# In each group of eight expert matmuls, the second expert goes first

## The chip, the cores and the metric

The kernel runs on one core of one Trainium2 chip. The metric is the device time of one execution in microseconds (us). Most executions of this kernel agree within 0.3%.

## The reference

A first block (token mixer, then a mixture of experts with 32 experts, 4 per token) is followed by a second block of two layers, whose feed-forward is a lookup over 16384 experts. Only the mixture of experts matters here. For 256 tokens of width 1024 in float32, cut down:

```
logits = yf @ router_w + router_b
top_val, top_idx = lax.top_k(logits, TOP_K)          # 4 of 32
gates = softmax(top_val)
def expert_block(xb, e):
    gt = minimum(xb @ w_gate[e] + b_gate[e], 7.0)
    up = clip(xb @ w_up[e] + b_up[e], -7.0, 7.0)
    return (gt * sigmoid(1.702 * gt) * (up + 1.0)) @ w_down[e] + b_down[e]
out = sum over the chosen experts of gate * expert_block
```

Each of `w_gate`, `w_up` and `w_down` is 1024 x 1024 for each expert: 12.6 MB an expert, 402.7 MB in all, read once.

## The kernel before

The generator `moe` holds the expert stage. Experts are taken in pairs. Each expert has up to `CAP` = 64 token slots; `xg` holds the gathered tokens, transposed. One expert alone therefore needs 64 of the array's 128 columns. The two experts of a pair share one PSUM bank `ps_g`: expert 0 writes partitions 0 to 63 from the left half of the array's columns (tile position (0, 0)), expert 1 partitions 64 to 127 from the right half ((0, 64)).

A weight tile `mo` is 128 x 2048 float32 (1 MB): 4 chunks of the contraction by 512 outputs of one matrix of one expert. It is loaded by `expert_load` (line 529, on SP's queue) into a ring of four buffers. A **group** is the work on two such tiles, one of each expert: eight matmuls, the two experts in turn, four chunks each. A pair of experts has 8 groups for gate and up (line 1055) and 4 for down (line 1089), so there are 192 groups, 384 weight tiles, 1536 matmuls. A float32 matmul stands as two MATMUL instructions in the profile, so these are 3072 there (2048 of line 1055 and 1024 of line 1089), and a pair of equal rows "x2" is one matmul of the program.

The order on every engine comes from the list scheduler that builds the program. It plays the program through on its own timeline and gives an engine the ready instruction of the best priority. While the expert stage runs, other work has a lower priority (the `filler` contexts): matmuls in float32r over all 128 columns for the context half of the second block, lines 209 to 211, 150 to 152, 671, 789, 897, 898 and 900. They are issued where the expert work is not ready by the scheduler's own times. Their weights come through SP's queue too (`wr`, lines 136 and 832), are split by ScalarE (`wh`, line 117) and VectorE (`wl`, line 118), and are used from there.

SP's queue runs in order: the load into a ring buffer waits until the last matmul that reads the buffer is done, and everything behind it in the queue waits too.

Of the kernel before, what the change touches and what calls it, by code (L numbers as in the profile page):

```python
# [64 lines left out]
def kernel(ctx: ExitStack, tc: tile.TileContext, a: dict, out: bass.AP):  # L65
# [88 lines left out]
    def xs_tiles(name, shape=None):  # L154
        h = xs.tile([P, KD * T], F32R, tag="xh", name=name + "h", bufs=2)
        l = xs.tile([P, KD * T], F32R, tag="xl", name=name + "l", bufs=2)
        return h, l
# [126 lines left out]
        nc.vector.tensor_add(b_, b_, h_)  # L284
        return gb

    # ---------------------------------------------------------------- modulation vectors of the second block
    modt = [[cp.tile([P, 2, 16], F32, name=f"modt{l}{q}") for q in range(3)] for l in range(2)]
    mrow = [[dr.tile([2, 2 * D], F32, name=f"mrow{l}{q}") for q in range(3)] for l in range(2)]

# [64 lines left out]
            return bank  # L355
        return f

    # ---------------------------------------------------------------- phase 1: attention of the first block
    X = xs_tiles("x")
    rp = pool("route", side="right")  # L360
    mg_stack = ctx.enter_context(ExitStack())
# [226 lines left out]
    for k2 in range(4):  # L588
        yb = ytr(k2)
        for c in range(2):  # L590
            k = 2 * k2 + c
# [89 lines left out]

    mg_stack.close()

    # ---------------------------------------------------------------- expert lookup layer: top-k, weights, dense passes
    def top16(rows):
        for s_, m_, _ in rows:
            nc.vector.max(m_[:, 0:8], s_)
        for s_, m_, x_ in rows:
            nc.vector.max_index(x_[:, 0:8], m_[:, 0:8], s_)
        for s_, m_, _ in rows:  # L690
            nc.vector.match_replace(s_, m_[:, 0:8], s_, LOWEST)
        for s_, m_, _ in rows:
            nc.vector.max(m_[:, 8:16], s_)
        for s_, m_, x_ in rows:
            nc.vector.max_index(x_[:, 8:16], m_[:, 8:16], s_)
# [229 lines left out]

    gds = [[dr.tile([P, 8, P, 16], F32, name=f"gd{i}{b}") for b in range(2)] for i in range(3)]

    # ---------------------------------------------------------------- experts of the first block
    def moe(mo, res):
        ahead = True  # L930
        lg = rp.tile([P, 2, 32], F32, name="lg")
# [76 lines left out]
        for g4 in range(8):  # L1008
# [11 lines left out]
            for k2 in range(4):  # L1020
                bank = psum("g").rearrange("p (c s) -> p c s", c=2)
                for c in range(2):
                    k = 2 * k2 + c
# [4 lines left out]
                for c in range(2):  # L1028
                    k = 2 * k2 + c
                    nc.scalar.activation(xg[:, k, :], bank[:, c, :], AF.Identity, bias=lnc[:, 1, k:k + 1], scale=lnc[:, 0, k:k + 1])  # L1030
            for p2 in range(2):
                e0 = 4 * g4 + 2 * p2
                selv = []
                for mi in range(2):
                    sel = mo.tile([P, 2, CAP], F32R, tag="sel", name="sel", bufs=4)
                    nc.vector.tensor_copy(sel, identr[:, 32 * mi + e0:32 * mi + e0 + 2, None].to_broadcast([P, 2, CAP]))
                    selv.append(sel.rearrange("p e s -> p (e s)"))
                if todo:
                    todo.pop()()
                hdn = mo.tile([P, D], F32, tag="hdn", name="hdn")  # L1040
                for hf in range(2):
                    banks = []
                    for mi, w in enumerate(("w_gate", "w_up")):
                        bank = psum("g")
                        for kq in range(2):
                            wt = []
                            for i in range(2):
                                if not (ahead and moq):
                                    res["last"] = expert_load(a[w][e0 + i, hf, kq])
                                    ahead = False  # L1050
                                wt.append(moq.pop(0))
                            for k in range(4):
                                for i in range(2):
                                    o = (2 * p2 + i) * CAP
                                    nc.tensor.matmul(bank[64 * i:64 * i + 64, :], xg[:, kq * 4 + k, o:o + CAP], wt[i][:, k, :],  # L1055
                                                     start=(kq == 0 and k == 0), stop=False, skip_group_check=True,
                                                     tile_position=(0, 64 * i))
                        nc.tensor.matmul(bank, selv[mi], bgr[:, hf * 512:hf * 512 + 512], start=False, stop=True,
                                         skip_group_check=True)
                        banks.append(bank)  # L1060
                    gt = mo.tile([P, 512], F32, tag="gt", name="gt", bufs=2)
                    nc.vector.tensor_scalar(gt, banks[0], 7.0, None, op0=ALU.min)
                    sg = mo.tile([P, 512], F32, tag="sg", name="sg", bufs=1)
                    nc.scalar.activation(sg, gt, AF.Sigmoid, scale=1.702)
                    up = mo.tile([P, 512], F32, tag="up", name="up", bufs=1)
                    nc.vector.tensor_scalar(up, banks[1], 7.0, -7.0, op0=ALU.min, op1=ALU.max)
                    nc.vector.tensor_mul(gt, gt, sg)
                    nc.vector.scalar_tensor_tensor(hdn[:, hf * 512:(hf + 1) * 512], up, 1.0, gt, op0=ALU.add, op1=ALU.mult)
                    yield
                if todo:  # L1070
                    todo.pop()()
                hT = mo.tile([P, KD, P], F32, tag="hT", name="hT", bufs=1)
                for c2 in range(2):
                    tp = psum("g").rearrange("p (c s) -> p c s", c=4)
                    for c in range(4):
                        k = 4 * c2 + c
                        nc.tensor.transpose(tp[:, c, :], hdn[:, k * P:(k + 1) * P], ident)
                    nc.scalar.activation(hT[:, 4 * c2:4 * c2 + 4, :], tp, AF.Copy)
                yo = mo.tile([P, D], F32, tag="y", name="yo")
                for hf in range(2):  # L1080
                    bank = psum("g")
                    for kq in range(2):
                        wt = []
                        for i in range(2):
                            res["last"] = expert_load(a["w_down"][e0 + i, hf, kq])
                            wt.append(moq.pop(0))
                        for k in range(4):
                            for i in range(2):
                                nc.tensor.matmul(bank[64 * i:64 * i + 64, :], hT[:, kq * 4 + k, 64 * i:64 * i + 64], wt[i][:, k, :],  # L1089
                                                 start=(kq == 0 and k == 0), stop=(kq == 1 and k == 3), skip_group_check=True,  # L1090
                                                 tile_position=(0, 64 * i))
                    nc.scalar.activation(yo[:, hf * 512:(hf + 1) * 512], bank, AF.Copy)
                tp = psum("g")
                pt_ = mo.tile([P, T], F32, tag="pt", name="pt", bufs=2)
                for tb in range(2):
                    nc.tensor.transpose(tp[:, tb * P:(tb + 1) * P], og[tb][:, 2 * p2:2 * p2 + 2, :].rearrange("p e s -> p (e s)"), ident)
                nc.scalar.activation(pt_, tp[:, 0:256], AF.Copy)
                for tb in range(2):
                    for hf in range(2):
                        bank = psum("g")  # L1100
                        nc.tensor.matmul(bank, pt_[:, tb * P:(tb + 1) * P], yo[:, hf * 512:(hf + 1) * 512], start=True, stop=True)  # L1101
                        nc.vector.tensor_add(acc[:, tb, hf * 512:(hf + 1) * 512], acc[:, tb, hf * 512:(hf + 1) * 512], bank)
                yield
# [67 lines left out]
    mo = pool("moe", stack=moe_stack)  # L1171
    mres = {}
    mgen = moe(mo, mres)
    next(mgen)
    general("g")
# [66 lines left out]
    moe_stack.close()  # L1242
    mow_stack.close()

    # ---------------------------------------------------------------- second block, first layer, latent tokens
    am_stack = ctx.enter_context(ExitStack())
    am = pool("amix", stack=am_stack)
    HA = xs_tiles("ha")
# [41 lines left out]
    vs_stack.close()  # L1290
    ra_stack.close()

    # ---------------------------------------------------------------- second block, second layer
    gl_stack = ctx.enter_context(ExitStack())
    gl = pool("gla", stack=gl_stack)
    wm_stack = ctx.enter_context(ExitStack())
# [248 lines left out]
            nc.sync.dma_start(out[:, tb, s_], o)  # L1545


# [1 line left out]
def consts():  # L1549
    p=np.arange(128)[:,None]; c=np.arange(128)[None,:]  # L1550
    ident=(p==c).astype(np.float32)
# [9 lines left out]
        tabs.append(np.where(ok,d,np.float32(1e30)).astype(np.float32))  # L1561
    return np.ascontiguousarray(np.concatenate([ident,iota,lt,gt,ones,trif,trib]+tabs,1))
def nt(w,n0=None):
    # [K,N] -> [N/128][128 p][K/128*128]
    K,N=w.shape
    return np.ascontiguousarray(w.reshape(K//128,128,N//128,128).transpose(2,1,0,3).reshape(N//128,128,K))
def tn(w,nw=512):
    # [K,N] -> [N/nw][K/256][128][2*nw]
    K,N=w.shape
    return np.ascontiguousarray(w.reshape(K//256,2,128,N//nw,nw).transpose(3,0,2,1,4).reshape(N//nw,K//256,128,2*nw))  # L1570
def xT(x):
# [3 lines left out]
def layout(i):  # L1575
# [10 lines left out]
    o['w_v1']=tn(np.ascontiguousarray(v[:,512:]),384)[0]  # L1586
    o['w_g']=np.stack([nt(ga),nt(gb)])
    o['sinks']=i['sinks']
    pa=i['w_proj_a'][0] # [256,1024] -> [2][128][4n][2k][128]
    o['w_pa']=np.ascontiguousarray(pa.reshape(2,128,2,4,128).transpose(2,1,3,0,4).reshape(2,128,1024))  # L1590
    o['w_pb']=nt(np.ascontiguousarray(i['w_proj_b'][0][perm]))
    o['w_out']=tn(i['w_out'][0])
# [55 lines left out]
```

## Time and profile before

| what | value |
|---|---|
| runs | 4312.46, 4317.56, 4323.53 us; median 4317.56 us |
| span of the profiled execution, first to last instruction | 4312.5 us |
| TensorE (PE) busy | 4173.2 us, 97% |
| VectorE (DVE), ScalarE (ACT) busy | 2385.2 us (55%), 1934.8 us (45%) |
| expert matmuls, lines 1055 and 1089, busy | 571.4 us and 289.7 us |
| first and last expert matmul starts | 309.7 us and 2237.8 us |

For the profiled execution the table has its span; that is within 0.1 us of the lowest run and 5.1 us below the median, and a time around the span is not shown apart from it. "PE busy" is the time in which at least one matmul is in the array. Matmuls overlap, so the start of one to the start of the next says what a matmul costs, and its own length does not.

### The profile page before, as it was taken

To read this page: it belongs to the slowest core of one execution; us is meant where nothing else is said; L and a number is where in the kernel's file an instruction comes from. 1 tells how busy PE (TensorE), PEld (TensorE's weight loads), DVE (VectorE), ACT (ScalarE), POOL (GpSimd) and SP (SyncE) were. 2 spreads that over 40 slices of the span, in tenths; PEclk is the share of its full clock that TensorE was granted. 3 is DMA by queue.
4 is the path that set the end of the run, shared out by engine and by line. 5 is a ranking of instruction groups with operands and counts; after the bars stand their busy time and mean duration, and the time that the engine had idled before them with its cause. 6 is when DMAs were issued, how large, how long until landed. Compare 5 with 4: busy or idle time off the path is not lost.

```text
span 4312.5 us, 63252 instructions
## 1 busy us (share of the span) xinstructions
PE 4173.2 (97%) x23786; PEld 3087.1 (72%) x23786; DVE 2385.2 (55%) x6357; ACT 1934.8 (45%) x2838; POOL 165.8 (4%) x230
## 2 busy tenths in 40 slices
PE   8999989999999999999998999999998989999998
PEld 7675545566565565656557999878877689988887
DVE  4364686433333333333337897655455689865555
ACT  5542246433232233323324497445544538754443
POOL 0000012000000000000000012000000002200000
PEclk9999999999999999999999999999998999999999
DMA  7658778887878878787875567876774345787773
GB/s 255 236 208 330 294 290 320 316 309 295 310 281 315 321 298 308 287 317 286 310 265 185 188 223 266 289 277 215 255 273 159 107 155 206 261 299 239 232 237 131
DMA packets 340046, 1115.49 MB, mean 259 GB/s; under 512 B 28934, under 2 KB 128006, under 8 KB 283672
## 3 DMA queue, kind: packets, MB, share of 16 engines
q1 hardware_dynamic: 323896, 1043.22, 67.5%
q10 hardware_dynamic: 15552, 66.07, 3.9%
q8 instruction: 190, 3.11, 0.3%
q0 software_dynamic: 288, 2.10, 0.1%
q14 instruction: 120, 0.98, 0.1%
HBM read 1041.97 MB, written 69.30 MB: 258 GB/s over the span
## 4 chain that ended last, share of the span: by engine, by line
PE 76%; DVE 5%; ACT 2%; DMA 2%; issue 1%; POOL 0%; SPq 0%; ACTq 0%; DVEq 0%; POOLq 0%
PE ps_g L1055 11%; PE ps_a L898 8%; PE ps_a L897 8%; PE ps_a L900 8%; PE ps_u L150 7%; PE ps_u L152 7%; PE ps_u L151 7%; PE ps_g L1089 6%; PE ps_a L789 3%; PE ps_g L1101 1%; DVE wl L118 1%; PE ps_g L329 1%; PE ps_g L209 1%; PE ps_g L210 1%; PE ps_g L211 1%; DVE o L788 1%
## 5 line engine op out<-in xcount | busy, mean ns | idle before, releaser
L118 DVE TENSOR_TENSOR wl<-wr,wh 128x1024 fp32r<-128x1024 f32 x933 | 1132.2, 1222 | 1126.6 <-ACT wh L117 1108.1
L117 ACT ACTIVATE wh<-wr 128x1024 fp32r<-128x1024 f32 x933 | 978.9, 1054 | 1379.1 <-PE ps_u L151 580.5
L898 PE MATMUL ps_a<-wl,ah 128*128 128x512 f32 x1536 | 590.5, 399 | 3.1 <-DVE wl L118 3.1
L1055 PE MATMUL ps_g<-mo,xg 128*64 128x512 f32 x2048 | 571.4, 603 | 10.0 <-DMA mo<-in_w_gate_dram 5.9
L897 PE MATMUL ps_a<-wh,ah 128*128 128x512 f32 x1536 | 577.6, 398 | 0.0
L900 PE MATMUL ps_a<-wh,al 128*128 128x512 f32 x1536 | 481.1, 396 | 0.0
L1055 PEld LDWEIGHTS ps_g<-mo,xg 128*64 128x64 f32 x2048 | 155.1, 137 | 286.6 <-issue 252.3
L897 PEld LDWEIGHTS ps_a<-wh,ah 128*128 128x128 f32 x1536 | 288.0, 188 | 85.2 <-issue 20.0
L898 PEld LDWEIGHTS ps_a<-wl,ah 128*128 128x128 f32 x1536 | 286.6, 188 | 82.3 <-issue 18.6
L900 PEld LDWEIGHTS ps_a<-wh,al 128*128 128x128 f32 x1536 | 286.4, 188 | 80.8 <-issue 16.4
L151 PE MATMUL ps_u<-xbl,wh 128*128 128x256 f32 x1088 | 315.4, 290 | 0.0
L150 PE MATMUL ps_u<-xbh,wh 128*128 128x256 f32 x1088 | 314.4, 289 | 0.0
L152 PE MATMUL ps_u<-xbh,wl 128*128 128x256 f32 x1088 | 313.7, 288 | 0.0
L1089 PE MATMUL ps_g<-mo,hT 128*64 128x512 f32 x1024 | 289.7, 605 | 2.4 <-DMA mo<-in_w_down_dram 2.4
L150 PE MATMUL ps_u<-xah,wh 128*128 128x256 f32 x960 | 276.5, 288 | 2.7 <-ACT sp L859 2.7
L152 PE MATMUL ps_u<-xch,wl 128*128 128x256 f32 x960 | 274.1, 287 | 4.2 <-DVE wl L118 4.2
L152 PE MATMUL ps_u<-xah,wl 128*128 128x256 f32 x960 | 274.5, 288 | 3.4 <-DVE wl L118 3.4
L151 PE MATMUL ps_u<-xal,wh 128*128 128x256 f32 x960 | 276.1, 288 | 0.0
L150 PE MATMUL ps_u<-xch,wh 128*128 128x256 f32 x960 | 274.5, 286 | 0.3 <-ACT wh L117 0.3
L151 PE MATMUL ps_u<-xcl,wh 128*128 128x256 f32 x960 | 274.6, 286 | 0.0
L788 DVE TENSOR_SCALAR o<-cst,it 128x128 f32<-128x128 f32 x768 | 233.7, 345 | 28.7 <-PE ps_a L789 28.2
L150 PEld LDWEIGHTS ps_u<-xbh,wh 128*128 128x128 f32 x1088 | 206.8, 190 | 48.3 <-issue 44.8
(652 smaller groups left out, 7028.1 us busy)
## 6 DMA issues: line engine op xcount, KB each, us to landing
wr<-in_p_u_dram SPq DMA_DIRECT2D x384, 512.0 KB, 4.6
wr<-in_p_v_dram SPq DMA_DIRECT2D x384, 512.0 KB, 4.5
mo<-in_w_gate_dram SPq DMA_DIRECT2D x128, 1024.0 KB, 7.1
mo<-in_w_up_dram SPq DMA_DIRECT2D x128, 1024.0 KB, 6.7
mo<-in_w_down_dram SPq DMA_DIRECT2D x128, 1024.0 KB, 7.1
gd<-stg ACTq DMA_DIRECT2D x48, 1024.0 KB, 6.2
gr<-gd SPq DMA_DIRECT2D x96, 512.0 KB, 7.0
mw<-in_w_mod_dram SPq DMA_DIRECT2D x48, 512.0 KB, 4.2
```

The source lines that it names most:

```text
L117: nc.scalar.activation(h, src, AF.Copy)
L118: return nc.vector.tensor_sub(l, src, h.bitcast(F32)).ins
L150: nc.tensor.matmul(o, wh, xh, start=first, stop=False)
L151: nc.tensor.matmul(o, wh, xl, start=False, stop=False)
L152: nc.tensor.matmul(o, wl, xh, start=False, stop=last)
L788: nc.vector.tensor_scalar(o1, iota, it[:, 0, t:t + 1], it[:, 2, t:t + 1], op0=ALU.is_equal, op1=ALU.mult)
L789: nc.tensor.matmul(bank[:, 2 * i2 + i, :], o2q[:, i, :], o1, start=True, stop=True)
L897: nc.tensor.matmul(acc[tb][hf], ah[:, ts], wh[:, hs], start=first, stop=False)
L898: nc.tensor.matmul(acc[tb][hf], ah[:, ts], wl[:, hs], start=False, stop=False)
L900: nc.tensor.matmul(acc[tb][hf], al[:, ts], wh[:, hf * 512:(hf + 1) * 512], start=False, stop=fin)
L1055: nc.tensor.matmul(bank[64 * i:64 * i + 64, :], xg[:, kq * 4 + k, o:o + CAP], wt[i][:, k, :], start=(kq == 0 and k == 0), stop=False, skip ...
L1089: nc.tensor.matmul(bank[64 * i:64 * i + 64, :], hT[:, kq * 4 + k, 64 * i:64 * i + 64], wt[i][:, k, :], start=(kq == 0 and k == 0), stop=(k ...
```

## The change

In both places the inner loop over the two experts is turned round. The loads, their order in the code, the products and the sums stay. (The rest of the diff takes comments out.)

```diff
@@ -1050,7 +1050,7 @@
                             for k in range(4):
-                                for i in range(2):
+                                for i in (1, 0):
                                     o = (2 * p2 + i) * CAP
                                     nc.tensor.matmul(bank[64 * i:64 * i + 64, :], xg[:, kq * 4 + k, o:o + CAP], wt[i][:, k, :],
@@ -1085,7 +1085,7 @@
                         for k in range(4):
-                            for i in range(2):
+                            for i in (1, 0):
                                 nc.tensor.matmul(bank[64 * i:64 * i + 64, :], hT[:, kq * 4 + k, 64 * i:64 * i + 64], wt[i][:, k, :],
```

Since the scheduler decides the order, the program changes more than the two lines do. On TensorE, in a group of the gate matrix early in the stage, `mo_3090` is the tile of the first expert, whose load is issued first, and `mo_3092` that of the second. Before:

```order
L1055 MATMUL ps_g_3089<-mo_3090,xg_2985 64x512
L209 MATMUL ps_a_3575<-wh_3614,hch_3465 128x512
L210 MATMUL ps_a_3575<-wl_3615,hch_3465 128x512
L211 MATMUL ps_a_3575<-wh_3614,hcl_3466 128x512
L1055 MATMUL ps_g_3089<-mo_3092,xg_2985 64x512
L1055 MATMUL ps_g_3089<-mo_3090,xg_2985 64x512
L1055 MATMUL ps_g_3089<-mo_3092,xg_2985 64x512
L1055 MATMUL ps_g_3089<-mo_3090,xg_2985 64x512
L1055 MATMUL ps_g_3089<-mo_3092,xg_2985 64x512
L1055 MATMUL ps_g_3089<-mo_3090,xg_2985 64x512
L1055 MATMUL ps_g_3089<-mo_3092,xg_2985 64x512
```

Now:

```order
L209 MATMUL ps_a_3575<-wh_3614,hch_3465 128x512
L210 MATMUL ps_a_3575<-wl_3615,hch_3465 128x512
L211 MATMUL ps_a_3575<-wh_3614,hcl_3466 128x512
L1055 MATMUL ps_g_3089<-mo_3092,xg_2985 64x512
L1055 MATMUL ps_g_3089<-mo_3090,xg_2985 64x512
L1055 MATMUL ps_g_3089<-mo_3092,xg_2985 64x512
L1055 MATMUL ps_g_3089<-mo_3090,xg_2985 64x512
L1055 MATMUL ps_g_3089<-mo_3092,xg_2985 64x512
L1055 MATMUL ps_g_3089<-mo_3090,xg_2985 64x512
L1055 MATMUL ps_g_3089<-mo_3092,xg_2985 64x512
L1055 MATMUL ps_g_3089<-mo_3090,xg_2985 64x512
```

The first expert's first matmul stood alone ahead of three matmuls of other work; it now stands with the other seven, at their place. The last matmul of the group now reads the first expert's tile.

In a group of the down matrix on TensorE (line 1089), `mo_5208` is the first expert's tile, `mo_5210` the second's, and line 789 is filler. Before:

```order
L1089 MATMUL ps_g_5207<-mo_5208,hT_5193 64x512
L789 MATMUL ps_a_8719<-o1_8736,o2_8730 128x128
L1089 MATMUL ps_g_5207<-mo_5210,hT_5193 64x512
L1089 MATMUL ps_g_5207<-mo_5208,hT_5193 64x512
L1089 MATMUL ps_g_5207<-mo_5210,hT_5193 64x512
```

Now:

```order
L1077 MATMUL ps_g_5200<-cst_75,hdn_5072 128x128 x4
L1089 MATMUL ps_g_5207<-mo_5210,hT_5193 64x512
L1089 MATMUL ps_g_5207<-mo_5208,hT_5193 64x512
L1089 MATMUL ps_g_5207<-mo_5210,hT_5193 64x512
L1089 MATMUL ps_g_5207<-mo_5208,hT_5193 64x512
```

The single filler matmul that parted the group stands elsewhere, and the group is whole. Over the whole program, the expert matmuls stand on TensorE in these uninterrupted runs (counted in the built order, in matmuls of the program):

| length of a run | 1 | 4 | 7 | 8 | 9 | 12 | 15 | 16 | 17 | 24 | runs |
|---|---|---|---|---|---|---|---|---|---|---|---|
| before | 141 | 0 | 143 | 24 | 3 | 0 | 2 | 8 | 1 | 0 | 322 |
| now | 0 | 5 | 0 | 169 | 0 | 5 | 0 | 5 | 0 | 1 | 185 |

TensorE has the same instructions as before, in another order, and outside the expert stage (the first 1748 rows and the last 11612 of 20877) the same order. The number of filler matmuls between the end of a group and the start of the next but one has the same median, 64. On SP's queue the two loads of a group stand side by side in 179 of 192 groups, before in 185.

## Rows read from the trace of the kernel before

**Rows 1.** The page: span, and part 1 (busy time and share).

```profile
span 4312.5 us, 63252 instructions
PE 4173.2 (97%) x23786; PEld 3087.1 (72%) x23786; DVE 2385.2 (55%) x6357; ACT 1934.8 (45%) x2838; POOL 165.8 (4%) x230
```

**Rows 2.** Busy time by stretch: length, engines with instructions, clock, DMA share, GB/s.

```profile
core 0: us, PE busy (x) PEld busy (x) DVE busy (x) ACT busy (x) POOL busy (x), PEclk, DMA share, GB/s
309.00:2242.00 1933.00, 1893.08 (x9328) 1107.14 (x9328) 798.90 (x2060) 661.49 (x923) 49.02 (x69) 0.99 0.81 305
309.00:460.00 151.00, 151.00 (x704) 85.75 (x705) 72.17 (x97) 47.08 (x57) 3.72 (x3) 1.00 0.84 323
460.00:800.00 340.00, 308.86 (x1603) 171.45 (x1598) 244.46 (x1360) 165.15 (x330) 45.30 (x67) 0.96 0.80 304
800.00:2000.00 1200.00, 1196.36 (x5893) 715.77 (x5893) 408.43 (x515) 380.34 (x451) 0.00 (x0) 1.00 0.82 305
```

**Rows 3.** Waits in the expert stage, all engines: us in total, times, longest us.

```profile
ACT wh L117 <- PE ps_u L151: 407.4, 107, 10.8
...
ACT wh L117 <- PE ps_a L900: 236.2, 90, 7.1
```

**Rows 4.** Timeline of PE around three groups: start us, us, instruction, count.

```profile
1106.31 3.65 PE L1089 MATMUL ps_g<-mo,hT 128*64 128x512 f32 x16
1109.89 0.39 PE L150 MATMUL ps_u<-xbh,wh 128*128 128x256 f32 x1
...
1111.30 0.28 PE L152 MATMUL ps_u<-xbh,wl 128*128 128x256 f32 x1
1111.42 0.28 PE L150 MATMUL ps_u<-xbh,wh 128*128 128x256 f32 x1
1111.63 1.07 PE L1089 MATMUL ps_g<-mo,hT 128*64 128x512 f32 x2
1112.63 0.38 PE L151 MATMUL ps_u<-xbl,wh 128*128 128x256 f32 x1
...
1114.29 0.28 PE L152 MATMUL ps_u<-xbh,wl 128*128 128x256 f32 x1
1114.50 3.65 PE L1089 MATMUL ps_g<-mo,hT 128*64 128x512 f32 x14
1118.07 0.39 PE L150 MATMUL ps_u<-xbh,wh 128*128 128x256 f32 x1
```

**Rows 5.** Timeline of PE: first and last lone matmul, last run of seven.

```profile
324.88 1.07 PE L1055 MATMUL ps_g<-mo,xg 128*64 128x512 f32 x2
...
2209.33 1.07 PE L1055 MATMUL ps_g<-mo,xg 128*64 128x512 f32 x2
...
2210.76 3.65 PE L1055 MATMUL ps_g<-mo,xg 128*64 128x512 f32 x14
```

**Rows 6.** The page, part 5: expert matmuls, busy us, mean ns, idle before.

```profile
L1055 PE MATMUL ps_g<-mo,xg 128*64 128x512 f32 x2048 | 571.4, 603 | 10.0 <-DMA mo<-in_w_gate_dram 5.9
...
L1089 PE MATMUL ps_g<-mo,hT 128*64 128x512 f32 x1024 | 289.7, 605 | 2.4 <-DMA mo<-in_w_down_dram 2.4
```

**Rows 7.** Waits of PE alone in the expert stage, for weight tiles.

```profile
PE ps_g L1055 <- DMA mo<-in_w_gate_dram: 5.9, 3, 3.9
...
PE ps_g L1055 <- DMA mo<-in_w_up_dram: 3.1, 3, 2.1
...
PE ps_g L1089 <- DMA mo<-in_w_down_dram: 2.4, 2, 1.6
```

**Rows 8.** Timeline of SP's queue: issues of weight tiles around the same groups.

```profile
1098.62 1.17 SPq L529 DMA_DIRECT2D mo<-in_w_down_dram  x2
...
1109.98 0.81 SPq L529 DMA_DIRECT2D mo<-in_w_down_dram  x2
...
1117.33 1.17 SPq L529 DMA_DIRECT2D mo<-in_w_down_dram  x2
```

**Rows 9.** The view of the tile `mo`: its transfers, issue to landing.

```profile
DMA to landing us min/median/max: 4.7/7.0/11.5
```

## The prediction

> **What bounds the kernel now.** I began with the page's busy shares: TensorE works 97% of the span and no other engine more than 55% [rows 1]. A mean hides stages, so I cut the span at the expert stage next. It takes 1933 us, and TensorE is busy in 1893 of them; between 800 and 2000 us it is idle for 3.6 of 1200, at a granted clock of 1.00, which is the 2.4 GHz level [rows 2]. The reader is to see that in this stretch only less work on TensorE, or a fuller array, can shorten the time. The waits say the same from the other side: ScalarE's split of the next filler weights stands idle until TensorE has freed a buffer, 407.4 and 236.2 us of the stage [rows 3], so that chain runs ahead of TensorE and is not what TensorE waits for. TensorE's own waits for expert weights come to 11.4 us in 3 + 3 + 2 = 8 of 192 groups [rows 7].
>
> **What an expert matmul costs.** I read this from the starts of the timeline. A whole group, 16 instructions, occupies TensorE from 1106.31 to 1109.89: 3.58 us. A lone matmul, 2 instructions, takes from 1111.63 to 1112.63: 1.00 us. The other seven, 14 instructions, take from 1114.50 to 1118.07: 3.57 us [rows 4]. So the eighth matmul beside seven is free and the same matmul alone costs a whole microsecond. The explanation that fits: the two experts sit in different halves of the array's columns and stream side by side, while two instructions of one expert follow each other in one half. Call the streaming of one instruction, with or without one in the other half, a slot. A lone matmul has 2 slots with the other half empty, eight alternating matmuls have 8 full slots, and seven, the second expert at both ends, also need 8. Per slot that is (3.58 - 1.00) / 6 = 0.43 us, and the rest of a run is 1.00 - 2 x 0.43 = 0.14 us. A run also delays its own start: the filler before it follows at 0.12 us (1111.30 to 1111.42) and the lone matmul only 0.21 us later (1111.63), so 0.09 us more [rows 4]. Each run thus costs 0.23 us beside its slots.
>
> The Trainium skill, TensorEngine Tiling (Array Packing), Overview and Key Properties, says that tiles of the array work independently and that a change of the tiling mode drains the array. The trace agrees on both: seven cost what eight do, and entering and leaving the mode costs 0.23 us; the page gives no size for the drain. By the drains alone the change would save the 31.5 us of the second term below, by the rows the empty half comes on top.
>
> **The change, part by part.** *Runs of expert matmuls.* A run of n matmuls has n slots if n is even and n + 1 if it is odd. The table of runs gives before 143 x 8 + 141 x 2 + 24 x 8 + 3 x 10 + 2 x 16 + 8 x 16 + 18 = 1826 slots in 322 runs. The 141 lone ones are in the trace too, from 324.88 to 2209.33 us [rows 5]. The sizes hold for the whole stage: 1826 x 0.43 + 322 x 0.23 = 859 us, and the two groups of rows are busy 571.4 + 289.7 = 861.1 us [rows 6]. Now there are 169 x 8 + 5 x 16 + 5 x 12 + 5 x 4 + 24 = 1536 slots in 185 runs, which is one per matmul: no half stays empty. Slots: -290 x 0.43 = -124.7 us. Runs: -137 x 0.23 = -31.5 us. Together -156 us on TensorE.
>
> *Second expert first.* That a run starts in the right half costs nothing of its own: the runs of seven already start there, and they are the 3.57 us.
>
> *The first expert's early matmul moves back to the others.* It was covered by no wait: it had its own microsecond on a busy engine. The group now starts when both tiles are there; the second tile's wait stands where it stood.
>
> *Buffers and SP's queue.* The first expert's tile is now read by the last matmul. Before, its load for the next group but one could be issued early: the pair at 1117.33 goes out 0.74 us before the run of seven ends at 1118.07, and takes 1.17 us to issue; after the run of eight that ends at 1109.89 it goes out at 1109.98 and takes 0.81 us [rows 4, 8]. So the first load is some 0.8 us later and the second up to 0.4 us. Behind it in SP's queue stand filler weights, whose users have the slack of [rows 3].
>
> *What is late next.* From the end of one group to the start of the next but one lies one whole group, and up to two removed lone matmuls of 1.00 + 0.09 us; the load gets 2.2 + 0.4 = 2.6 us less. A transfer takes 4.7 to 11.5 us, median 7.0 [rows 9]. For the run at 1114.50 the loads were issued from 1098.62 on [rows 8]; the second lands by the median near 1106.5 and at the slowest near 1111, 8 or 3.5 us early. So the usual group keeps its cover and the tight ones lose it. Bounds: nothing (no wait grows) to 156 us (every group waits 0.81 us more, and all is lost). I take 20 us: three times as many groups waiting as now, at the same 1.4 us, would be 23 us more, and the example lies nearer to the lower end.
>
> *Transfers as a whole.* The stage moves 1933 us x 305 GB/s = 590 MB [rows 2]. In 1933 - 136 = 1797 us that is 328 GB/s. The stretch from 309 to 460 us ran at 323 GB/s and 0.84 of the transfer engines while TensorE was busy in all of its 151.00 us [rows 2], so at least 323 is to be had without a stall.
>
> The Trainium skill, DMA: Bandwidth & Descriptors, Measured, gives 341 GB/s for a transfer of 1 MB, the size of these tiles. No run here has shown that as a ceiling; if it were one, 590 MB would need 1730 us, an estimate from the page that leaves only 67 us between transfers and TensorE. It is the best reason against the change that I found.
>
> *Outside the stage* the order is the same on TensorE and nothing changes.
>
> **Sum.** 4312.5 - 156 + 20 = 4176.5 us against the profiled span. The median of the runs is 5.1 us above that span, so about 4181 us; I say 4180.
>
> **Rivals.**
> - *Transfers bind.* If the stage cannot go past the 323 GB/s seen, it takes 590 / 323 = 1826 us, saves 107, and the median is 4211 us; if it stops half way between 305 and 323 GB/s, at 314, it saves 54: 4263 us. For it: a share of 0.81 to 0.84 already. Against it: 11.4 us of waits.
> - *TensorE is not what sets the stage where the lone matmuls are.* Between 460 and 800 us it is idle 31 us and VectorE works 244 of 340 us [rows 2]. If that stretch kept its length, 340 / 1933 of the gain, 27 us, is lost and the median is about 4208 us. If it held for the whole stage the time would stay at 4317 us, but then the 1200 us with 3.6 us idle could not be there.
> - *Slower: the loads become the pace.* With both loads of a group issued only after the last matmul of the group two before, every group could end up waiting. The point from which it decides is 156 / 192 = 0.81 us more wait per group; at 1.2 us it is 192 x 1.2 - 156 = 74 us slower, 4392 us. Against it: 8 waits in 192 groups, and 3.5 us or more in hand in the example.
> - *The change does nothing to TensorE's order.* The built order speaks against it; its chance is inside the 4317 us case.
>
> **How the numbers follow.** The forecast's own case, losses of 0 to some 45 us out of 156, is 4156 us (by the span, nothing lost) to 4207 us (by the median): 75%. Transfers that bind, or waits that take more than half: 13%, 4207 to 4290 us. No gain: 5%. Slower: 4%. A gain beyond the sum, should the 11.4 us of waits go too, below 4150 us: 3%. The range 4150 to 4228 us holds the first case and a good third of the second, about 8 in 10. What a measurement of this kernel can tell from no change is about 0.3%, 13 us (its three runs span 11 us). Faster by more: 75 + 13 + 3 = 91%. Within: 5%. Slower: 4%.
>
> **What would show it.** In the changed profile the lines 1055 and 1089 should be busy about 861 - 156 = 705 us together, with no pair "x2" alone in the timeline and groups of 3.58 us. The stage should end near 2106 us instead of 2242, the rows after it unchanged but earlier. The stage's rate should be near 328 GB/s, the waits for `mo` near 30 us, and TensorE still busy more than 95% of it. The prediction is wrong if the waits for `mo` come to 60 us or more, if groups of eight that start in the right half take more than 3.6 us, or if the busy time falls and idle time of equal size appears behind filler weights.

## The result and the profile after

The changed kernel took 4170.72 us (median of 4 runs, 4166.39 to 4176.07) against 4315.03 us before (4 runs): ratio 0.9665, 95% interval 0.9644 to 0.9685, so 3.4% or 144 us faster. The forecast was 4180 us, 4150 to 4228.

The page of the changed kernel, span and busy time, then its two groups of expert matmuls, as in [rows 1] and [rows 6]:

```profile
span 4166.2 us, 63176 instructions
PE 4009.8 (96%) x23786; PEld 3059.7 (73%) x23786; DVE 2382.3 (57%) x6357; ACT 1928.0 (46%) x2835; POOL 166.6 (4%) x230
...
L1055 PE MATMUL ps_g<-mo,xg 128*64 128x512 f32 x2048 | 474.5, 606 | 17.7 <-DMA mo<-in_w_gate_dram 11.5
...
L1089 PE MATMUL ps_g<-mo,hT 128*64 128x512 f32 x1024 | 238.7, 609 | 6.3 <-DMA mo<-in_w_down_dram 6.2
```

The span fell by 4312.5 - 4166.2 = 146.3 us. TensorE's busy time fell by 163.4 us and its idle time rose from 139.3 to 156.4, by 17.1. The expert matmuls alone went from 861.1 to 713.2 us, with the same number of instructions. VectorE and ScalarE did the same work in a shorter span.

The stretches of the changed kernel, as in [rows 2]; the first row is its expert stage, cut at 2097:

```profile
core 0: us, PE busy (x) PEld busy (x) DVE busy (x) ACT busy (x) POOL busy (x), PEclk, DMA share, GB/s
309.00:2097.00 1788.00, 1731.12 (x9339) 1083.44 (x9336) 798.06 (x2063) 655.96 (x918) 50.08 (x69) 0.99 0.88 330
309.00:460.00 151.00, 146.26 (x718) 85.63 (x715) 76.28 (x101) 45.74 (x54) 7.30 (x5) 0.98 0.92 354
460.00:800.00 340.00, 294.86 (x1632) 170.37 (x1631) 239.57 (x1355) 163.26 (x331) 42.78 (x64) 0.94 0.81 310
800.00:2000.00 1200.00, 1198.39 (x6521) 775.02 (x6518) 450.05 (x566) 420.18 (x504) 0.00 (x0) 1.00 0.89 333
```

TensorE is still what is busy: 1198.39 of 1200 us between 800 and 2000. The same 1200 us now hold 6521 matmul instructions in place of 5893, and the transfers run at 333 GB/s in place of 305 without holding it up there. The new idle time is earlier: 45 us between 460 and 800, where there were 31, and 4.7 us before 460, where there was none.

The timeline of TensorE in the changed kernel, two groups; the answer to [rows 4]:

```profile
1044.97 3.65 PE L1089 MATMUL ps_g<-mo,hT 128*64 128x512 f32 x16
1048.56 0.39 PE L151 MATMUL ps_u<-xbl,wh 128*128 128x256 f32 x1
...
1055.09 3.65 PE L1089 MATMUL ps_g<-mo,hT 128*64 128x512 f32 x16
1058.67 0.50 PE L897 MATMUL ps_a<-wh,ah 128*128 128x512 f32 x1
```

Groups stand whole and take 3.59 and 3.58 us; no lone pair is left anywhere in the trace, whose 185 runs have the lengths of the built order.

TensorE's waits in the expert stage of the changed kernel (total us, times, longest), as in [rows 7]:

```profile
PE ps_g L1055 <- DMA mo<-in_w_gate_dram: 11.5, 5, 4.7
PE ps_g L1101 <- DVE xst L1102: 10.0, 1, 10.0
...
PE ps_g L1089 <- DMA mo<-in_w_down_dram: 6.2, 3, 2.5
PE ps_g L1055 <- DMA mo<-in_w_up_dram: 6.2, 3, 2.8
```

The waits for weight tiles went from 11.4 us in 8 groups to 23.9 us in 11. The one wait of 10.0 us for `xst` was 2.1 us before.

SP's queue in the changed kernel, the loads after the two groups above, as in [rows 8]:

```profile
1048.65 0.81 SPq L529 DMA_DIRECT2D mo<-in_w_down_dram  x2
...
1058.76 0.80 SPq L529 DMA_DIRECT2D mo<-in_w_down_dram  x2
```

Both loads of a pair now go out just after the group has ended, in 0.8 us, as after the whole group of [rows 8]. Counted in the two traces, the first load of a pair went out some 0.8 us ahead of the group's end in 144 of 190 groups before, and in none now.

### The profile page after: what moved, and what is told of

Read it like the earlier page. It is cut to its first block, busy times and chain, and to the rows that moved or that the text cites. A ratio compares the mean times of both kernels' runs of the same rounds, so it can differ in the third digit from the quotient of the medians.

```text
span 4166.2 us, 63176 instructions
## 1 busy us (share of the span) xinstructions
PE 4009.8 (96%) x23786; PEld 3059.7 (73%) x23786; DVE 2382.3 (57%) x6357; ACT 1928.0 (46%) x2835; POOL 166.6 (4%) x230
## 4 chain that ended last, share of the span: by engine, by line
PE 72%; DVE 5%; ACT 2%; DMA 2%; issue 1%; POOL 0%; ACTq 0%; SPq 0%; DVEq 0%; POOLq 0%
PE ps_a L898 9%; PE ps_a L897 9%; PE ps_a L900 9%; PE ps_u L150 8%; PE ps_u L151 8%; PE ps_g L1055 8%; PE ps_u L152 8%; PE ps_g L1089 4%; PE ps_a L789 2%; PE ps_g L1101 1%; DVE wl L118 1%; PE ps_g L329 1%; PE ps_g L209 1%; PE ps_g L210 1%; PE ps_g L211 1%
## 5 line engine op out<-in xcount | busy, mean ns | idle before, releaser
L117 ACT ACTIVATE wh<-wr 128x1024 fp32r<-128x1024 f32 x933 | 979.8, 1055 | 1270.3 <-PE ps_u L151 500.1
L1055 PE MATMUL ps_g<-mo,xg 128*64 128x512 f32 x2048 | 474.5, 606 | 17.7 <-DMA mo<-in_w_gate_dram 11.5
L898 PEld LDWEIGHTS ps_a<-wl,ah 128*128 128x128 f32 x1536 | 286.4, 188 | 76.1 <-issue 11.4
L1055 PEld LDWEIGHTS ps_g<-mo,xg 128*64 128x64 f32 x2048 | 138.2, 138 | 272.2 <-issue 243.5
L1089 PE MATMUL ps_g<-mo,hT 128*64 128x512 f32 x1024 | 238.7, 609 | 6.3 <-DMA mo<-in_w_down_dram 6.2
L789 PE MATMUL ps_a<-o,o 128*128 128x128 f32 x1536 | 226.9, 278 | 14.2 <-ACT o L784 10.1
```

The costliest lines, as they stand in the source:

```text
L117: nc.scalar.activation(h, src, AF.Copy)
L789: nc.tensor.matmul(bank[:, 2 * i2 + i, :], o2q[:, i, :], o1, start=True, stop=True)
L898: nc.tensor.matmul(acc[tb][hf], ah[:, ts], wl[:, hs], start=False, stop=False)
```

## The experiments

Theory A: the gain comes from expert matmuls standing whole on TensorE. A group is parted when its leading matmul reads the tile that lands first; then a half of the columns streams while the other is empty. Theory B: starting in the right half, or with that expert, is what helps. Theory C: the gain is a by-product of filler that the scheduler moved. Theory D: lone matmuls are dear only because TensorE enters and leaves the half-width mode for them.

### Which of the two: the half, or the tile that lands last

Both kernels turn the loads round, in the two loops and in the loads ahead of the stage; the second also has the matmuls of the changed kernel. One of the two loops, cut:

```diff
-                            for i in range(2):
+                            for i in (1, 0):
                                 if not (ahead and moq):
                                     res["last"] = expert_load(a[w][e0 + i, hf, kq])
                                     ahead = False
-                                wt.append(moq.pop(0))
+                                wt[i] = moq.pop(0)
```

Loads turned, matmuls as before the change:

> The first expert goes first again in every group, as before the change, but now the second expert's weight tile is loaded first. Theory A (the gain comes from expert matmuls that stand whole on TensorE, because the group starts with the tile that lands last): the built order has no lone matmul, 1536 slots in 182 runs, so expert busy time near 713 us as in the changed kernel and a time of 4171 us, within 15. Theory B (the gain comes from starting in the right half of the array, or from that expert): the time goes back to about 4315 us.

Loads and matmuls turned:

> The second expert goes first and its tile is loaded first as well. Theory A: the leading matmul is ready before its partner again; the built order has 144 lone matmuls and 147 runs of seven, 1832 slots in 328 runs, so expert busy time near 861 us and 4318 us, within 15. Theory B: starting in the right half is what helps, so about 4171 us.

Measured: 4154.53 us (ratio 0.9628, 0.9612 to 0.9644) for the first, 1.5 us below the range of theory A, and 4306.97 us (0.9988, 0.9979 to 0.9998) for the second, inside it. The page of the kernel with the loads turned:

```profile
L1055 PE MATMUL ps_g<-mo,xg 128*64 128x512 f32 x2048 | 468.8, 601 | 13.3 <-DMA mo<-in_w_up_dram 9.8
L1089 PE MATMUL ps_g<-mo,hT 128*64 128x512 f32 x1024 | 237.9, 607 | 10.6 <-DMA mo<-in_w_down_dram 6.9
```

and of the kernel with both turned:

```profile
L1055 PE MATMUL ps_g<-mo,xg 128*64 128x512 f32 x2048 | 578.1, 604 | 9.7 <-DMA mo<-in_w_gate_dram 5.8
L1089 PE MATMUL ps_g<-mo,hT 128*64 128x512 f32 x1024 | 290.5, 602 | 2.2 <-DMA mo<-in_w_down_dram 2.2
```

The timeline of the latter has the lone matmuls and the runs of seven again:

```profile
1002.81 1.07 PE L1055 MATMUL ps_g<-mo,xg 128*64 128x512 f32 x2 [0.88 <-DMA mo<-in_w_up_dram]
...
1006.75 3.65 PE L1055 MATMUL ps_g<-mo,xg 128*64 128x512 f32 x14
```

Theory B has fallen: the kernel that starts in the left half has the whole gain, and the one that starts in the right half with the tile that is loaded first has almost none. What counts is that the leading matmul reads the tile that is loaded last.

### One part alone

Gate and up alone (the first of the two edits):

> Only the groups of gate and up (line 1055) are turned round. Theory A: 1638 slots in 233 runs, by 0.43 us a slot and 0.23 us a run 102 us less than before, times 144 / 156 (what the whole change gave against its count) 94 us: 4221 us, within 12. Theory C (the gain is a by-product of filler that the scheduler moved): no relation to the count, half of the gain with each part, about 4243 us, or any other value.

Down alone (the second edit):

> Only the groups of down (line 1089) are turned round. Theory A: 1732 slots in 277 runs, 51 us less than before by the count, times 144 / 156 47 us: 4268 us, within 12. Theory C: about 4243 us, or any other value; the two parts need not add up to 144 us.

Measured: 4214.50 us (0.9771, 0.9754 to 0.9787) and 4263.82 us (0.9883, 0.9866 to 0.9899), against 4313.14 us for the kernel before, run beside them: 98.6 and 49.3 us, together 147.9, where the whole change gave 144. Theory C has no reason for parts that add up and that each lie within 5 us of the count. It has fallen for the gain as a whole; differences of some 15 us between orders with the same count remain (below).

### Halves or mode

The experts one after the other in a group (the first of two places):

```diff
-                            for k in range(4):
-                                for i in (1, 0):
+                            for i in (1, 0):
+                                for k in range(4):
```

> The loop over the experts is put outside the loop over the four chunks: four matmuls of the second expert, then four of the first. The products, the loads and the groups stay. The built order has 191 runs, 1524 of the 1536 matmuls in runs of eight or more that start where they did. Theory A (two experts stream side by side in the two halves, and an empty half costs the slot): a group has 15 to 16 slots in place of 8, so 1344 to 1536 slots more, 578 to 660 us more on TensorE, and 4750 to 4830 us. Theory D (a lone matmul is dear because of entering and leaving the mode, and the halves have nothing to do with it): as many runs as in the changed kernel, so 4171 us, within 15.

Measured: 4471.24 us (2 runs; ratio 1.0373, 1.0352 to 1.0394), 300 us over the changed kernel with about as many runs. Theory D has fallen: whole runs are dear too when the halves don't take turns. The size was missed by about half, and the timeline of that kernel says why:

```profile
703.69 0.83 PE L789 MATMUL ps_a<-o,o 128*128 128x128 f32 x6
704.45 5.42 PE L1055 MATMUL ps_g<-mo,xg 128*64 128x512 f32 x16
709.80 0.71 PE L789 MATMUL ps_a<-o,o 128*128 128x128 f32 x4
```

The group takes 5.35 us, 12 slots of 0.43 and not 15 or 16. How many of its instructions are in the array at a time is seen in four short stretches of the same run (busy us, instructions present, clock, DMA share, GB/s):

```profile
704.94:705.36 0.42, 0.42 (x2) 1.00 0.60 254
705.37:705.79 0.42, 0.42 (x2) 1.00 0.51 215
...
707.14:707.50 0.36, 0.36 (x4) 1.00 0.99 410
...
708.43:708.85 0.42, 0.42 (x2) 1.00 0.19 78
```

An instruction is 0.59 us long and the next in its half starts 0.43 us after it, so one half at work shows 2 in a slot and both halves 4. In the middle of the group both work. By the starts in the trace, the first expert's matmuls begin with the fifth of the second expert's eight instructions (706.23 and 706.22 us), while three of those are still to come: 4 slots alone, 4 together, 4 alone. With 12 slots a group, 192 x 12 x 0.43 + 191 x 0.23 = 1035 us; the two lines are busy 688.1 + 346.9 = 1035.0 us in its profile.

### The price of a run

Each weight tile is loaded in two transfers, and most groups fall apart into two runs of four:

```diff
-        ins = nc.sync.dma_start(w_.rearrange("p k f -> p (k f)"), src).ins
+        for c in range(2):
+            ins = nc.sync.dma_start(w_[:, 2 * c:2 * c + 2, :].rearrange("p k f -> p (k f)"), src[:, 1024 * c:1024 * c + 1024]).ins
```

> The changed kernel, with each weight tile loaded by two transfers of 512 KB in place of one of 1 MB. The built order has 1536 slots as in the changed kernel, but in 297 runs in place of 185, most of them of four matmuls. Theory A with the run's own price of 0.23 us: 112 x 0.23 = 26 us more on TensorE, expert busy near 739 us, and 4197 us, within 12 (less if the smaller transfers land earlier and take some of the 24 us of waits away). If only slots cost and a run has no price: 4171 us.

Measured: 4194.48 us (0.9734, 0.9718 to 0.9750), 24 us over the changed kernel where 26 was expected. The expert matmuls are busy 487.7 + 245.3 = 733.0 us, and TensorE in all 4042.7, 32.9 us more than in the changed kernel. A run of four, in that kernel's timeline (its line 1056 is line 1055 elsewhere), lasts 1.87 us up to the next row, 4 x 0.43 + 0.15:

```profile
999.69 1.94 PE L1056 MATMUL ps_g<-mo,xg 128*64 128x512 f32 x8
1001.56 0.50 PE L899 MATMUL ps_a<-wl,ah 128*128 128x512 f32 x1
1001.90 0.39 PE L898 MATMUL ps_a<-wh,ah 128*128 128x512 f32 x1
1002.12 0.40 PE L899 MATMUL ps_a<-wl,ah 128*128 128x512 f32 x1
```

So a run has a price of its own beside the slots, and it is more than the 0.23 us of the prediction. The first filler matmul behind the run holds TensorE for 0.34 us (1001.56 to 1001.90), the next for 0.22 (1001.90 to 1002.12). Against its like elsewhere, the first one takes 0.10 us more: that is the median over 123 runs of this trace between 800 and 2000 us, and over 147 in the kernel before. That makes 0.33 us a run, 37 us for 112 runs. TensorE lost 32.9; nearly 5 us of the rest lie in the clock (next section). In the time only 24 us show, because idle time fell by 7.7 us, so that the agreement with 26 is partly chance.

### What the transfers still cost

Half of each weight tile is left out, and the matmuls read the other half twice (cut):

```diff
-        ins = nc.sync.dma_start(w_.rearrange("p k f -> p (k f)"), src).ins
+        ins = nc.sync.dma_start(w_[:, 0:2, :].rearrange("p k f -> p (k f)"), src[:, 0:1024]).ins
...
-    xg[:, kq * 4 + k, o:o + CAP], wt[i][:, k, :],
+    xg[:, kq * 4 + k, o:o + CAP], wt[i][:, k % 2, :],
```

> The changed kernel, but each weight tile has only its first two chunks loaded, and the matmuls of chunks 2 and 3 read chunks 0 and 1 again: half of the experts' 403 MB isn't read, and the sums are those of other weights. Slots are the same, 1536 in 172 runs. It asks what the transfers still cost. The prediction's view (transfers cost the changed kernel only the waits for weight tiles, 24 us in the stage): 20 to 35 us less, 4136 to 4151 us. If the transfers set the stage at its 330 GB/s: more than 60 us less, below 4110 us.

Measured: 4130.72 us (0.9586, 0.9570 to 0.9602), 40 us under the changed kernel: more than the 20 to 35 of the prediction's view, less than the 60 that would have meant that transfers set the stage. The page of that kernel shows where: TensorE busy 3989.9 us, 19.9 less, and idle for 4126.3 - 3989.9 = 136.4, 20.0 less. Its expert matmuls are busy 698.8 us, 14.4 less, with 1536 slots as well and 13 runs fewer (3 us). The rest is TensorE's clock. Two groups of the changed kernel, the second behind a wait for its tile:

```profile
610.47 3.65 PE L1089 MATMUL ps_g<-mo,hT 128*64 128x512 f32 x16
...
617.93 5.35 PE L1089 MATMUL ps_g<-mo,hT 128*64 128x512 f32 x16 [2.50 <-DMA mo<-in_w_down_dram]
```

The first group's stretch, and a part of the second's (columns as in [rows 2]):

```profile
610.47:614.05 3.58, 3.58 (x18) 1.05 (x17) 3.58 (x33) 0.00 (x0) 1.18 (x2) 1.00 0.89 325
...
618.80:622.20 3.40, 3.40 (x11) 1.19 (x9) 3.40 (x37) 1.48 (x6) 0.00 (x0) 0.51 0.81 342
```

The second group takes 5.28 us up to the next row and not 3.58, and no idle time lies inside it: the granted clock fell to 0.50, the 1.2 GHz level, soon after the wait of 2.50 us. The changed kernel has eight such stretches in its expert stage, each in or behind waits of TensorE, and seven runs lie partly in them: 40.8 us, where runs of these lengths elsewhere take 28.5, so 12.3 us more. With half of the bytes it is one run and 1.1 us, with two loads a tile 7.7 us, in the kernel before about 5.5 us. A wait for a weight tile thus costs more than its idle time.

The kernel with half of the bytes also has another order, as the scheduler counts on earlier loads. That the whole 40 us are the transfers' is therefore not shown, only that they are not much more.

### A version beyond the change

The kernel with the loads turned was the fastest so far. On it, the same idea for the modulation vectors: both tiles are loaded ahead of four matmuls in the four quarters of the columns, and the tile loaded last leads (cut to the loop):

```diff
-                    for j in (2 * j2, 2 * j2 + 1):
+                for j in (2, 0, 3, 1):
```

> The first expert goes first and the second's tile is loaded first (the order of the run that turned the loads alone), and the same idea in the modulation vectors (line 329): there four matmuls in four quarters of the array's columns read two tiles; both tiles are now loaded ahead of the four, and the matmul of the tile that is loaded last goes first. Theory A: some of that line's 35 us of busy time goes, 5 to 15 us, but only where TensorE sets the pace; the first stage, where half of them stand, is 92% busy. So 4140 to 4155 us. If nothing there is on the path: 4155 us, within 8.

Measured: 4171.65 us (0.9679, 0.9663 to 0.9695), outside both ranges, and 13 to 17 us slower than the two measurements without it (4158.75 below, 4154.53 above). In its profile, TensorE is as busy as in the kernel with the loads turned alone (4006.6 against 4007.5 us) and idle for 162.3 us against 148.6: line 329's two groups were busy 29.6 + 29.7 us in place of 36.8 + 30.6, but its waits for its tiles rose from 4.7 to 8.6 us, and those for tiles of `w_up` from 9.8 to 19.5. The idea did not carry to that place.

The two kernels with whole groups, side by side:

> The changed kernel once more, beside the one with only the loads turned, on the same chip: is the mirror really faster by the 16 us that separate the two medians (4170.7 and 4154.5)? If yes: 4165 to 4175 us here and 4150 to 4160 us there. If that was spread between runs and chips: the two within 6 us of each other.

> The kernel with only the loads turned (first expert first, second's tile loaded first), once more, beside the changed kernel. If it is faster by itself: 4150 to 4160 us, and 10 us or more below the changed kernel. By theory A alone, which counts slots and runs (1536 in 182 against 1536 in 185), the two should differ by 1 us; a lasting difference is then one of waits, whose cause these runs don't show.

Measured: the changed kernel 4173.12 us (0.9680, 0.9667 to 0.9693), the one with the loads turned 4158.75 us (0.9646, 0.9633 to 0.9659). The difference of 14 us lasts, and the count (1 us) does not explain it. The stretches of the changed kernel in that run,

```profile
460.00:820.00 360.00, 310.51 (x1715) 176.24 (x1711) 242.70 (x1362) 167.59 (x336) 43.52 (x65) 0.95 0.83 311
820.00:2000.00 1180.00, 1180.00 (x6425) 765.95 (x6427) 446.81 (x561) 414.68 (x496) 0.00 (x0) 1.00 0.89 333
```

and of the kernel with the loads turned,

```profile
460.00:820.00 360.00, 319.36 (x1781) 186.20 (x1779) 250.80 (x1372) 175.21 (x345) 40.80 (x64) 0.96 0.86 327
820.00:2000.00 1180.00, 1180.00 (x6437) 764.03 (x6435) 445.32 (x555) 410.88 (x491) 0.00 (x0) 1.00 0.88 333
```

put 9 us of it into the idle time between 460 and 820 us (49.5 against 40.6), in waits that are scattered over several lines. In the whole stage the waits for weight tiles are 26.7 against 18.9 us, and those for `xst` 9.5 against 5.0. The two orders differ throughout that stretch. Which difference does it stays open.

## Why the prediction was right, point by point

Seven kernels against the count of slots and runs, in us (the medians are from three batches, in which the kernel before took 4312 to 4315 us):

| kernel | slots | runs | 0.43 x slots + 0.23 x runs | lines 1055 and 1089 busy | median time |
|---|---|---|---|---|---|
| before | 1826 | 322 | 859 | 861.1 | 4315.0 |
| both turned | 1832 | 328 | 863 | 868.6 | 4307.0 |
| down alone | 1732 | 277 | 808 | 808.8 | 4263.8 |
| gate and up alone | 1638 | 233 | 758 | 761.4 | 4214.5 |
| two loads a tile | 1536 | 297 | 729 | 733.0 | 4194.5 |
| changed | 1536 | 185 | 703 | 713.2 | 4170.7 |
| loads turned | 1536 | 182 | 702 | 706.7 | 4154.5 |

Left out are the kernel with the experts one after the other, whose 12 slots a group were read from its own trace, and the one with half of the bytes, which moves less (1536 slots, 172 runs: 700 us counted, 698.8 busy, 4130.7 us). The busy time of the two lines has neither the 0.09 us in front of a run nor the 0.10 us behind it, and counts 0.07 us of modelled end (a group is busy for 3.65 us and followed after 3.58), so that 0.23 us a run fits it is in part chance.

- *What bounds the kernel.* Right: the time follows the expert matmuls' busy time down the whole table, but for the scatter of some 15 us between orders (the first two rows go opposite ways by 8 us).
- *Slots and runs.* Right in kind and near in size, with two errors that partly cancel. The sum was 156 us on TensorE; the two lines lost 147.9 us and TensorE as a whole 163.4 us. The price of a run left out the 0.10 us on the first filler behind it: with 0.33 us, 137 runs are 45 us in place of 31.5, and the sum is 170. And the forecast had no term for the clock: about 7 us of expert matmuls more at the 1.2 GHz level (12.3 against 5.5), which leaves 163. The 10 us by which the changed kernel's lines exceed their count are this slower clock too.
- *Second expert first costs nothing.* Right: groups take 3.58 us, in the median of the changed kernel and of the kernel with the loads turned, which starts in the left half.
- *Buffers and SP's queue.* Right: both loads now leave after the group, within 0.81 us.
- *What is late next.* 20 us were taken, of bounds from 0 to 156. Idle time rose by 17.1 us. Its make-up was not as put: the waits for weight tiles grew by 12.5 us, in 11 groups and not in 24, and one wait for `xst` by 10.0 less 2.1. That the total came so near is therefore partly luck, and the slower clock behind such waits was not foreseen. A transfer of a weight tile now took 7.5 us in the median and at most 12.9, in place of the times in [rows 9].
- *Transfers as a whole.* 328 GB/s were forecast for the stage and 330 measured, so the rival that stops at 323 has fallen. The stretch up to 460 us ran at 354 GB/s, above the 323 that served as a bound; there TensorE idled for 4.7 us. The Trainium skill, DMA: Bandwidth & Descriptors, Measured, gives 341 GB/s for a transfer of 1 MB. By the 354 GB/s of this stretch it is no ceiling for many of them at once.
- *The stretch from 460 to 800 us.* The rival that feared for it was right in part: of the 17.1 us of new idle time about 14 lie there. It did not take the 27 us that it was given.
- *Outside the stage.* Right: from the start of the last expert matmul to the end the changed kernel took 4166.2 - 2089.1 = 2077.1 us, before 4312.5 - 2237.8 = 2074.7.
- *Sum.* -163.4 + 17.1 = -146.3 on the span, where -156 + 20 = -136 was forecast. The range was said to hold a good third of the case from 4207 to 4290 us; up to 4228 it is 21 of 83 us, a quarter, which hardly changes its chance.

## What to carry to other kernels

Where several tiles feed one group of matmuls and a scheduler places each instruction when it is ready, let the leading matmul read the tile that is loaded last: the group then starts whole. Count the uninterrupted runs in the built order, and price one from the starts in the timeline (a lone one, a whole one, and the first filler behind each); the length of an instruction and the busy share of 97% hid 148 of the expert matmuls' 861 us. Orders with equal counts can still differ by 15 us here, so a second way to get the same runs is worth a run.

## What the runs showed of the hardware

- Two column halves work side by side even if one expert's instructions all stand ahead of the other's in the program: the second half began when three of the eight instructions of the first were still to come, and the group took 12 slots, not 15 or 16. Only four instructions (two matmuls of float32) at each end were alone.
- A run of half-width matmuls among full-width ones costs about 0.33 us beside its streaming: 0.09 us in front of it, 0.14 in it, and 0.10 on the first full-width matmul behind it. 112 more runs made TensorE 32.9 us busier, with the same slots and some 5 us less at the lower clock.
- The waits of TensorE on weight tiles also show in its busy time, through the clock: behind a wait of 2.50 us the granted clock fell to 0.50, and a group took 5.28 us in place of 3.58. With half of the bytes, 14 us of the expert matmuls' busy time went, of which the count of runs explains 3 and the clock 11.
